# A decoder step on one core: the bank reads of four decays, low parts in quarters, and the place of three gate projections

## The chip, the core and the metric

The kernel runs on one core of a Trainium2 chip. What counts is its device time in microseconds (us). Before the change three runs took 1305.10, 1305.83 and 1306.04 us: a median of 1305.83.

The engines are named as in the profile: TensorE (PE, with its weight loads as PEld), VectorE (DVE), ScalarE (ACT), GpSimd (POOL) and SyncE (SP), which here issues DMAs. Each runs its own instructions in order and waits on semaphores for the others.

## What is computed

One layer of a hybrid decoder on 16 learned tokens, 256 prompt tokens and 8 sequences of 8 new tokens. All of them lie side by side as columns: 336 in a projection, of which 320 are kept as two chunks of 128 and a last strip of 64.

```python
def trunk_layer(x, conf_buf, mconv_buf, h0, segments, p):
    ...
    xn = rmsnorm(x, norm1_w)
    proj = xn @ w_in + b_in
    cuts = np.cumsum([2 * C_CONV, D_INNER, CONV_DIM, M_HEADS])
    glu_in, z, xbc, dt_raw, gate_raw = jnp.split(proj, [int(c) for c in cuts], axis=-1)

    ga, gb = jnp.split(glu_in, 2, axis=-1)
    u = ga * jax.nn.sigmoid(gb)
    conf_cat = jnp.concatenate([conf_buf.astype(u.dtype), u], axis=1)
    c = causal_depthwise(conf_cat, conf_dw_w, conf_dw_b)
    c = jax.nn.silu(layernorm(c, conf_ln_g, conf_ln_b))
    y_a = c @ w_conf_out + b_conf_out
    ...
    y = gated_group_rmsnorm(y.reshape(b, T, D_INNER), z, m_norm_w)
    y_b = y @ w_m_out

    g_a, g_b = jnp.split(jax.nn.sigmoid(gate_raw), 2, axis=-1)
    x = x + (g_a * y_a + g_b * y_b) @ w_o
    x = x + peer(rmsnorm(x, norm2_w), peer_w_q, peer_keys, peer_u, peer_v)
```

The `y` in the middle comes from a recurrence of 32 heads in 8 groups of 4. Within a chunk it is computed with a matrix of decays:

```python
        acs = jnp.cumsum(dtc * Ag, axis=1)
        seg = acs[:, :, None] - acs[:, None, :]
        decay = jnp.exp(jnp.where(causal[None, :, :, None, None], seg, -jnp.inf))
        cb = jnp.einsum('btgn,bsgn->btsg', Cc, Bc)
        dx = dtc[..., None] * xc
        y_diag = jnp.einsum('btsgr,bsgrp->btgrp', cb[..., None] * decay, dx)
        y_off = jnp.einsum('btgn,bgrpn->btgrp', Cc, hc) * jnp.exp(acs)[..., None]
        ...
        st = jnp.einsum('bsgn,bsgrp->bgrpn', Bc, w_end[..., None] * dx)
        h_new = jnp.exp(last)[..., None, None] * hc + st
```

`peer` is the expert stage: each token picks 16 of 16384 experts in each of 8 heads, and their rows of two tables are weighted and summed.

## The kernel before

**Weights.** A projection uses a weight block of 128x1024, fetched by SyncE into `wraw` (four buffers) and split in two: a high part `wh`, a copy by ScalarE (L243, "CAST"), and a low part `wl` = `wraw` - `wh`, by GpSimd (L247) or now and then by VectorE. `wh` and `wl` have two buffers each, so a block's parts are made while the projections before it still run. `proj` is 16 matmuls with `wh` (against the high and the low part of the activations, `ah` and `al`) and then 8 with `wl`. The results lie in banks named `pj`, three of them. `split` can cut the low part into `parts` pieces:

```python
                (nc.gpsimd if on_pool else nc.vector).tensor_tensor(l[:, q:q + m], src[:, q:q + m],
...
            split(h, l, raw, on_pool=not on_dve, on_dve=lm[0] == 1, parts=1 if lm[0] else 4)
```

`lm[0]` is the share of blocks whose low part VectorE makes. It is 0 in one stage alone, the projection `w_q` ahead of the experts: there, and nowhere else, GpSimd works in quarters.

**The mixer.** A loop goes over the eight groups g = 0 to 7. Each turn runs projections for the next group as tasks: the convolution branch's value and its gate half (`xnf` is the sigmoid of the gate half, `ccat` the product of both with its history, `ch` a copy of it for the convolution of 31 taps, which runs as pairs of a ScalarE product and a VectorE sum into `pcv`), four for x, B and C (`mcat`), then two for z (`sz`). After each task a generator of the group's recurrence, `ssd(g)`, takes one step, and the group before takes one of its last ones. The steps, with the names in the traces:

1. copies with `spread_in` (`ptr<-cst,spr`), `decay(0)`, `decay(1)`
2. `turn(0)`, `decay(2)`, `decay(3)`
3. `turn(1)`, `turn(2)`, small copies into `cz`
4. `running()`: `pq`, whose result ScalarE copies to `gs`, and `st` times `el` on GpSimd; `inner(0)`; `Bm`
5. `inner(1)`, `state(0)`; 6. `inner(2)`, `state(1)`; 7. `state(2)`, `out(0)`; 8. `out(1)`
9. the squares `sq` and the update of `st`; 10. the sum of squares `pgn`

`decay(r)` spreads one head's `acs` over 128 rows by a matmul into a bank `pdec` (L629). VectorE takes it in three pieces (64 or 128 columns, L631) into `dec`, ScalarE takes half of its rows into `e2` (`e` in the trace) with the exponential (L635), and after every second head ScalarE takes the exponential of a pair of `dec` in place (L637). `pdec` has two banks, shared with `py`, `po` and `pgb` (tag "y"). VectorE and ScalarE read a bank of `pdec` one after the other, in the order in which the program names them. `turn(i)` transposes three blocks into `ptr`, from which come `xt` and `wx`. `inner(i)` makes `pcb` and multiplies `dec` by it (L660, VectorE). `state(i)` makes `pst` and from it `hs`. `ptr`, `pq`, `pcb` and `pst` share two banks (tag "misc"): `pst` of `state(0)` takes the bank that the first `pcb` leaves, and `pq` that of the second `ptr`.

In the last turn (g = 7) eight gate projections take the place of the next group's tasks, with the convolution branch's layer norm between them: `norm_mean` and `norm_scale`, and `norm_apply`, where VectorE multiplies the buffers `cbuf` by `rs` (L841). `conf_out(0)` and `conf_out(1)` follow, with gates `gs`.

Behind the loop come the group norm's statistics, `conf_out(2)` to `(5)` (low parts on VectorE), and a loop over the groups: `gnorm` spreads a group's scale into a bank `pgb` and VectorE multiplies `xg` by it (L775, two instructions), `gsplit` cuts the result into `yh` and `yl`. `conf_out(6)` and `(7)` stand behind groups 1 and 3, and three gate projections behind the loop. Then `w_mo` (two blocks for an output), `w_o`, `w_q` and the expert stage: the tables' blocks `eraw`, read with 512 KB a DMA on two queues, go through TensorE (`in_uT`, L1417, then `in_vE`, L1519), while rows gathered by GpSimd's indirect DMAs (`wuv`) go through VectorE.

**What sets the order.** Up to the three gates each matmul is pinned, so TensorE keeps the program's order:

```python
        pin = [True]
        def mm(*a_, **kw):
            i_ = nc.tensor.matmul(*a_, **kw)
            if pin[0]:
                tc.keep_in_program_order(i_)
```

ScalarE's functions that need a table (`act`) are chained in the program's order too. All else is put in order by a scheduler. A function whose table isn't loaded gets an `ACT_TABLE_LOAD` ahead of it: the exponential and the sigmoid need different ones.

Of the kernel before, what the change touches and what calls it, by code (L numbers as in the profile page):

```python
# [61 lines left out]
NW0 = 3  # L62
# [96 lines left out]
def body(tc, ia, oa, stop=None):  # L159
    nc = tc.nc  # L160
    with ExitStack() as top:
# [13 lines left out]
# [4 lines that stand above are left out]
# [39 lines left out]
        def act(out, in_, f, **kw):  # L218
            i_ = nc.scalar.activation(out, in_, f, **kw)  # L219
            chain(i_)  # L220
            return i_
# [20 lines left out]
        def split(h, l, src, on_pool=False, on_dve=False, parts=1):  # L242
            (nc.vector.tensor_copy if on_dve else nc.scalar.copy)(h, src)  # L243
            n = src.shape[1]
            m = n // parts if on_pool and len(src.shape) == 3 else n
            for q in range(0, n, m):
                (nc.gpsimd if on_pool else nc.vector).tensor_tensor(l[:, q:q + m], src[:, q:q + m],  # L247
                                                                    h[:, q:q + m].bitcast(F32), op=OP.subtract)
# [22 lines left out]
        def weight(src, i):  # L271
            raw = wp.tile([128, KD, 128], F32, name="wraw", bufs=rb[0])
            nc.sync.dma_start(raw, src[i].rearrange("p (k m) -> p k m", m=128))
            h = wp.tile([128, KD, 128], F32R, name="wh", bufs=2)
            l = wp.tile([128, KD, 128], F32R, name="wl", bufs=2)
            nw[0] += 1
            f_ = lm[0]
            on_dve = int((nw[0] + 1) * f_) > int(nw[0] * f_)
            split(h, l, raw, on_pool=not on_dve, on_dve=lm[0] == 1, parts=1 if lm[0] else 4)
            return h, l  # L280

        lm, nw = [LM[3]], [NW0]

        def rows(h, l):
            return lambda k: (h[:, k, :], l[:, k, :])
# [331 lines left out]
        def ssd(g, xg, bc, sz):  # L617
# [8 lines left out]
            def decay(r):  # L626
                h = 4 * g + r
                pb = ps.tile([128, T], F32, name="pdec", tag="y", bufs=2)[:, :T2]
                mm(pb, id3[:, h:h + 1].to_broadcast([128, 128]), acs3[:, :T2], start=True, stop=True)  # L629
                for i, (t0, L) in enumerate(OTILES):  # L630
                    nc.vector.scalar_tensor_tensor(dec[:, r, t0:t0 + L], pb[:, t0:t0 + L], acs[i][:, h:h + 1],  # L631
                                                   mneg[:, t0:t0 + L], op0=OP.add, op1=OP.add)
                hs_ = slice(r % 2 * 64, r % 2 * 64 + 64)
                act(e2[hs_, r // 2], pb[hs_], AF.Exp)
                if r % 2:  # L635
                    act(dec[:, r - 1:r + 1], dec[:, r - 1:r + 1], AF.Exp)

# [80 lines left out]
            yield  # L718
            turn(0)
            decay(2)  # L720
            decay(3)
            yield
            turn(1)
            turn(2)
            for s_ in range(2):
                nc.scalar.copy(cz[:, 4 * s_:4 * s_ + 4, 8 * s_:8 * s_ + 8],
                               CT[:, SQ + 32 * s_:SQ + 32 * s_ + 32].rearrange("p (q t) -> p q t", q=4))
# [69 lines left out]
        def gate():  # L797
            n = len(gates)
            j = 2 * n if n < KD else 2 * (n - KD) + 1
            p = project(64 + j, xo)[:, :T2]  # L800
            s = gate_tile(n)
            nc.scalar.activation(s, p, AF.Identity, bias=V("b_in", 64 + j))  # L802
            gates.append(s)
# [74 lines left out]
        for g in range(G):  # L878
            new = ssd(g, *tiles, sz)
            if g + 1 < G:  # L880
                tiles, steps = xbc(g + 1)
                tasks = conf(g + 1) + steps
            else:
                lm[0] = LM[1]
                tasks = [gate] * 8
            run(old, 1)
            run(new, 1)
            for n, f in enumerate(tasks):
                f()
                run(old, 1)  # L890
                run(new, 1)
                if g + 1 == G:
                    if n == 0:
                        norm_mean()
                    elif n == 3:
                        norm_scale()
                    elif n in (4, 5):
                        norm_apply(range(4 * n - 16, 4 * n - 12))
            if g + 1 < G:
                sz, zsteps = zproj(g + 1)  # L900
                zsteps[0]()
                run(new, 1)
                zsteps[1]()
                old = new
            else:
                for j in range(2):
                    conf_out(j)
                    run(new, 1)
# [9 lines left out]
        for g in range(G):  # L918
            gnorm(g, r24[0])
            gsplit(g)  # L920
            if g % 2 and g < 4:
                conf_out(6 + g // 2)
        for _ in range(3):
            gate()
        pin[0] = False
        lm[0] = LM[2]
        mh = m2.tile([128, KD, T2], F32R, name="mh")
        ml = m2.tile([128, KD, T2], F32R, name="ml")

# [234 lines left out]
        for t in qTs:  # L1164
            nc.gpsimd.memset(t[:, T2:], 0.0)
        lm[0] = 0.0
        fetched = []
        pres = [ExitStack(), ExitStack()]

# [485 lines left out]
```

## Time and profile before

| | before |
|---|---|
| runs, median (lowest to highest) | 1305.83 us (1305.10 to 1306.04) |
| the profiled execution | 1305.18 us, of which the span is 1303.3 us |
| mean granted clock of TensorE | 0.993 |
| TensorE busy | 97% |
| VectorE, GpSimd, ScalarE busy | 74%, 45%, 40% |
| moved by DMA | 373.77 MB, 287 GB/s |

The span reaches from the first to the last instruction; 1.9 us of the execution lie around it. A percentage is an average over stages that differ: the mixer to about 430 us, where VectorE, ScalarE and GpSimd are all busy, then `w_mo`, `w_o` and `w_q`, and from about 800 us on the expert stage, in which the DMA engines are nearly full. In rows of the timeline a time is counted from the span's start, and in square brackets stands how long the engine had been idle and what released it.

### The profile page before, as it was taken

The numbers are of one execution on the slowest core, as the hardware profiler recorded it, in microseconds if no ns is written. First come the engines' busy times: TensorE is split into PE (matmuls) and PEld (weight loads), VectorE is DVE, ScalarE is ACT, GpSimd is POOL, SyncE is SP. The second block draws the span as 40 slices with busy tenths as digits, with TensorE's granted clock in tenths as the row PEclk, the third lists the DMA queues.
The fourth block names the chain that finished last, engine by engine and source line by source line (L and its number), as shares of the span: only waits on it lengthen the run. The fifth ranks groups of instructions, "written<-read, shape, count | busy, mean of one in ns | idle before, by whom it ended". The sixth has DMA issues, their size and how long they took to land.

```text
span 1303.3 us, 23601 instructions
## 1 busy us (share of the span) xinstructions
PE 1261.8 (97%) x8951; PEld 1216.5 (93%) x8951; DVE 961.0 (74%) x2095; ACT 521.9 (40%) x1332; POOL 584.2 (45%) x553
## 2 busy tenths in 40 slices
PE   9999999999889999999999899999999999999997
PEld 7989888898779999999999898999999999999997
DVE  6888778977987335548999967788788888544444
ACT  6878876787665444634222221112211111001102
POOL 2587777886673656975122222233332222122210
PEclk9999999999999999999999999899999999999999
DMA  6444454344424344765989999999999999999992
GB/s 247 172 145 160 169 187 166 137 168 154 148 95 160 138 149 146 262 228 187 379 321 416 415 415 415 415 412 416 414 415 415 414 415 415 397 416 415 413 411 110
DMA packets 85905, 373.77 MB, mean 287 GB/s; under 512 B 10000, under 2 KB 15376, under 8 KB 66208
## 3 DMA queue, kind: packets, MB, share of 16 engines
q1 hardware_dynamic: 48336, 166.82, 34.4%
q0 software_dynamic: 19584, 142.62, 26.7%
q10 hardware_dynamic: 17872, 62.84, 12.0%
q8 instruction: 70, 1.15, 0.3%
q14 instruction: 43, 0.35, 0.1%
HBM read 359.18 MB, written 13.06 MB: 286 GB/s over the span
## 4 chain that ended last, share of the span: by engine, by line
PE 81%; DMA 7%; DVE 7%; ACT 4%; issue 1%; POOL 0%; DVEq 0%; ACTq 0%; SPq 0%; POOLq 0%
PE pj L176 29%; PE va L1519 25%; PE pj L1417 17%; DMA eraw<-in_uT_dram 3%; DMA wuv<-in_peer_uv_dram,gid 3%; PE pg L1445 1%; PE pst L176 1%; ACT L219 1%; ACT wh L243 1%; PE po L176 1%; PE psc L1195 1%; DVE pcv L519 1%; PE py L176 1%; DVE st L712 1%; ACT e L219 1%
## 5 line engine op out<-in xcount | busy, mean ns | idle before, releaser
L1149 POOL DMA_INDIRECT wuv<-in_peer_uv_dram,gid x136 | 166.5, 1225 | 490.1 <-PE va L1519 118.8
L247 POOL TENSOR_TENSOR wl<-wraw,wh 128x1024 fp32r<-128x1024 f32 (+1 forms) x160 | 278.3, 1753 | 129.0 <-ACT wh L243 79.1
L1519 PE MATMUL va<-S,eraw 128*128 128x184 f32 x2048 | 325.6, 320 | 0.0
L1519 PEld LDWEIGHTS va<-S,eraw 128*128 128x128 f32 x2048 | 318.9, 190 | 0.9 <-issue 0.9
L1417 PE MATMUL pj<-nd,eraw 128*128 128x184 f32 x1792 | 293.5, 323 | 9.6 <-DMA eraw<-in_uT_dram 8.4
L1417 PEld LDWEIGHTS pj<-nd,eraw 128*128 128x128 f32 x1792 | 281.2, 191 | 11.1 <-issue 8.7
L176 PE MATMUL pj<-ah,wh 128*128 128x336 f32 (+1 forms) x768 | 241.8, 326 | 1.2 <-ACT gs L802 0.9
L176 PE MATMUL pj<-al,wh 128*128 128x336 f32 (+1 forms) x768 | 231.9, 315 | 0.0
L1315 DVE SCALAR_TENSOR_TENSOR ygat<-wuv,scg,ygat 128x1024 f32<-128x1024 f32 x128 | 164.0, 1281 | 90.8 <-ACT scg L1310 90.6
L1307 ACT ACTIVATE scg<-scg 128x1 f32<-128x1 f32 x136 | 27.3, 202 | 437.9 <-DVE wuv L1305 317.8
L1305 DVE SCALAR_TENSOR_TENSOR wuv<-wuv,x2m 128x1024 f32<-128x1024 f32 x128 | 156.3, 1221 | 48.8 <-DMA wuv<-in_peer_uv_dram,gid 47.9
L243 ACT CAST wh<-wraw 128x1024 fp32r<-128x1024 f32 x125 | 130.9, 1048 | 97.0 <-PE pj L176 78.9
L176 PEld LDWEIGHTS pj<-ah,wh 128*128 128x128 f32 x768 | 145.1, 189 | 7.0 <-issue 2.5
L176 PEld LDWEIGHTS pj<-al,wh 128*128 128x128 f32 x768 | 144.7, 189 | 0.7
L519 DVE SCALAR_TENSOR_TENSOR pcv<-ch,vec,pcv 128x320 f32<-128x320 f32 x232 | 127.7, 550 | 18.6 <-ACT pcv L517 16.0
L176 PE MATMUL pj<-ah,wl 128*128 128x336 f32 (+1 forms) x768 | 137.3, 315 | 0.0
L176 PEld LDWEIGHTS pj<-ah,wl 128*128 128x128 f32 x768 | 119.9, 188 | 0.6 <-POOL wl L247 0.3
L1419 ACT ACTIVATE S<-pj 128x184 f32<-128x184 f32 x128 | 37.8, 315 | 89.6 <-PE pj L1417 89.2
L530 DVE SCALAR_TENSOR_TENSOR pj<-mcat,vec,pj 128x360 f32<-128x360 f32 x96 | 56.5, 591 | 3.4 <-ACT pj L528 3.1
L219 ACT ACT_TABLE_LOAD x31 | 39.8, 1283 | 19.5 <-DVE dec L631 19.0
L1456 DVE SCALAR_TENSOR_TENSOR S<-pg,S 128x232 f32<-128x232 f32 (+1 forms) x92 | 34.7, 417 | 13.1 <-PE pg L1445 13.1
L1417 PE MATMUL pj<-nd,pre 128*128 128x184 f32 x256 | 42.0, 319 | 0.0
(388 smaller groups left out, 1701.8 us busy)
## 6 DMA issues: line engine op xcount, KB each, us to landing
wraw<-in_w_in_dram SPq DMA_DIRECT2D x80, 512.0 KB, 3.2
eraw<-in_vE_dram SPq DMA_DIRECT2D x64, 512.0 KB, 10.2
eraw<-in_vE_dram ACTq DMA_DIRECT2D x64, 512.0 KB, 10.3
eraw<-in_uT_dram SPq DMA_DIRECT2D x60, 512.0 KB, 10.2
eraw<-in_uT_dram ACTq DMA_DIRECT2D x52, 512.0 KB, 10.1
st<-in_state_dram SPq DMA_DIRECT2D x8, 1024.0 KB, 5.0
out_ssm_s_dram<-st SPq DMA_DIRECT2D x8, 1024.0 KB, 5.0
wraw<-in_w_mo_dram SPq DMA_DIRECT2D x16, 512.0 KB, 3.2
```

Source lines behind the costliest of these rows:

```text
L176: i_ = nc.tensor.matmul(*a_, **kw)
L219: i_ = nc.scalar.activation(out, in_, f, **kw)
L243: (nc.vector.tensor_copy if on_dve else nc.scalar.copy)(h, src)
L247: (nc.gpsimd if on_pool else nc.vector).tensor_tensor(l[:, q:q + m], src[:, q:q + m], h[:, q:q + m].bitcast(F32), op=OP.subtract)
L519: nc.vector.scalar_tensor_tensor(to, in_, sc, eights(acc), op0=OP.mult, op1=OP.add)
L530: nc.vector.scalar_tensor_tensor(o, cat[:, w:w + n], wv, o, op0=OP.mult, op1=OP.add)
L1149: i_ = nc.gpsimd.indirect_dma_start(out=u, out_offset=None, in_=ia["peer_uv"], in_offset=bass.IndirectOffsetOnAxis(ap=gid[:, c:c + 1], axi ...
L1305: nc.vector.scalar_tensor_tensor(u[:, :D], u[:, :D], 1.0, x2m if c < NPICK else x2e, op0=OP.mult, op1=OP.mult, accum_out=w)
L1315: nc.vector.scalar_tensor_tensor(a_, u[:, D:], scg[:, c:c + 1], a_, op0=OP.mult, op1=OP.add)
L1417: i_ = nc.tensor.matmul(p[:, :ND], raw[:, k, :], nd[:, k, :], start=(k == 0), stop=(k == KD - 1))
L1419: nc.scalar.activation(Sv(b), p[:, :ND], AF.Gelu)
L1519: i_ = nc.tensor.matmul(va[k // 2][:, k % 2], raw[:, k, :], Sv(b), start=(b == 0 and k % 2 == 0), stop=(b == 127), skip_group_check=True)
```

## The change

It has three parts and removes no matmul.

- In `decay` ScalarE's exponential into `e2` is named ahead of VectorE's three reads, and `decay(3)` moves from the second step of `ssd` to the third, behind `turn(1)` and `turn(2)`.
- The count of pieces of a low part is a variable, `quarters`: 1 at the start, 4 from the last group's tasks on, 1 again from `w_mo` on, and 4 as before at `w_q`.
- Of the three gate projections behind the norm's loop one now stands in it, behind group 5; the other two stand behind group 7, where they were.

```diff
-            split(h, l, raw, on_pool=not on_dve, on_dve=lm[0] == 1, parts=1 if lm[0] else 4)
+            split(h, l, raw, on_pool=not on_dve, on_dve=lm[0] == 1, parts=quarters[0])
...
-        lm, nw = [LM[3]], [NW0]
+        lm, nw, quarters = [LM[3]], [NW0], [1]
...
                 mm(pb, id3[:, h:h + 1].to_broadcast([128, 128]), acs3[:, :T2], start=True, stop=True)
+                hs_ = slice(r % 2 * 64, r % 2 * 64 + 64)
+                act(e2[hs_, r // 2], pb[hs_], AF.Exp)
                 for i, (t0, L) in enumerate(OTILES):
                     nc.vector.scalar_tensor_tensor(dec[:, r, t0:t0 + L], pb[:, t0:t0 + L], acs[i][:, h:h + 1],
                                                    mneg[:, t0:t0 + L], op0=OP.add, op1=OP.add)
-                hs_ = slice(r % 2 * 64, r % 2 * 64 + 64)
-                act(e2[hs_, r // 2], pb[hs_], AF.Exp)
                 if r % 2:
...
             turn(0)
             decay(2)
-            decay(3)
             yield
             turn(1)
             turn(2)
+            decay(3)
...
                 lm[0] = LM[1]
+                quarters[0] = 4
                 tasks = [gate] * 8
...
                 conf_out(6 + g // 2)
-        for _ in range(3):
-            gate()
+            elif g % 2:
+                for _ in range(g // 2 - 1):
+                    gate()
         pin[0] = False
         lm[0] = LM[2]
+        quarters[0] = 1
...
         lm[0] = 0.0
+        quarters[0] = 4
```

**ScalarE in one of the groups 0 to 6.** Before, from the third and fourth reads of `pdec` on:

```order
L219 ACTIVATE e_2774<-pdec 64x320 x2
L219 ACTIVATE dec<-dec 128x640
L243 CAST wh<-wraw 128x1024
L219 ACT_TABLE_LOAD
L219 ACTIVATE xnf<-pj,vec 128x336
L646 COPY xt_2933<-ptr 128x128
L646 COPY xt_2942<-ptr 128x128
L537 COPY cnew<-ccat 128x30
L499 COPY ch<-ccat 128x1216
L537 COPY cnew<-ccat 128x240
L501 COPY ch<-ccat 128x304
L243 CAST wh<-wraw 128x1024
```

And after, from the cast behind `Bm` on (the third read of `pdec` and three `Bm` stand ahead of it):

```order
L243 CAST wh<-wraw 128x1024
L219 ACT_TABLE_LOAD
L219 ACTIVATE xnf<-pj,vec 128x336
L646 COPY xt_2926<-ptr 128x128
L646 COPY xt_2935<-ptr 128x128
L219 ACT_TABLE_LOAD
L219 ACTIVATE e_2774<-pdec 64x320
L537 COPY cnew<-ccat 128x30
L499 COPY ch<-ccat 128x1216
L537 COPY cnew<-ccat 128x240
L501 COPY ch<-ccat 128x304
L219 ACTIVATE dec<-dec 128x640
```

The fourth read stands behind `xnf` and the copies of `xt`, with a table load of its own, and the exponential of the second pair of `dec` has come from ahead of `xnf` to behind the copies of `ch`. In the built program one table load has been added in each of the groups 0 to 6; the last group has no `xnf`.

**TensorE at the norm's spreads, groups 5 and 6.** Before (`acs_4957` is the scale that is spread, `id_566` the selector, and a gate projection is the row of `ah`, `al` and eight `wl`):

```order
L176 MATMUL pj<-ch,wl 128x320 x8
L176 LDWEIGHTS id_566
L176 MATMUL pgb<-acs_4957,id_566 128x320
L176 LDWEIGHTS id_566
L176 MATMUL pgb<-acs_4957,id_566 128x320
L176 LDWEIGHTS id_566
L176 MATMUL pgb<-acs_4957,id_566 128x320
L176 LDWEIGHTS id_566
L176 MATMUL pgb<-acs_4957,id_566 128x320
L176 MATMUL pj<-ah,wh 128x320
```

And after, from the end of the gate that now stands between them:

```order
L176 MATMUL pj<-ah,wl 128x320 x8
L176 LDWEIGHTS id_566
L176 MATMUL pgb<-acs_4987,id_566 128x320
L176 LDWEIGHTS id_566
L176 MATMUL pgb<-acs_4987,id_566 128x320
L176 MATMUL pj<-ah,wh 128x320
L176 MATMUL pj<-al,wh 128x320
```

The spreads of groups 4 and 5 follow `conf_out(7)`, then comes a whole gate projection, and those of groups 6 and 7 come behind it.

**GpSimd in the last group.** Before (`wx` and `hs` are those of `turn` and `state`, `st` is `running`'s):

```order
L650 TENSOR_TENSOR wx_4511<-xt_4508,wd 128x256
L650 TENSOR_TENSOR wx_4520<-xt_4517,wd 128x256
L681 TENSOR_TENSOR st<-st,el 128x256 x4
L247 TENSOR_TENSOR wl<-wraw,wh 128x1024
L681 TENSOR_TENSOR st<-st,el 128x256 x4
L247 TENSOR_TENSOR wl<-wraw,wh 128x1024
L669 TENSOR_TENSOR hs_4672<-hs_4620,el 128x256
L247 TENSOR_TENSOR wl<-wraw,wh 128x1024
L669 TENSOR_TENSOR hs_4730<-hs_4672,el 128x256
```

And after:

```order
L650 TENSOR_TENSOR wx_4510<-xt_4507,wd 128x256
L650 TENSOR_TENSOR wx_4519<-xt_4516,wd 128x256
L247 TENSOR_TENSOR wl<-wraw,wh 128x256 x4
L681 TENSOR_TENSOR st<-st,el 128x256 x8
L247 TENSOR_TENSOR wl<-wraw,wh 128x256 x4
L669 TENSOR_TENSOR hs_4687<-hs_4632,el 128x256
L247 TENSOR_TENSOR wl<-wraw,wh 128x256 x4
L669 TENSOR_TENSOR hs_4748<-hs_4687,el 128x256
```

Each low part is four instructions of 256 columns instead of one of 1024, and one of them has moved ahead of the eight `st`. Over the whole program GpSimd's 96 full low parts become 82, and its 64 quarters become 120: fourteen low parts are made in quarters that were not.

## The prediction, made before the changed kernel was run

> **What bounds the kernel now.** I read the page first, then TensorE's waits, then the timeline of one group, of the last group and of the norm spreads. The page's busy line and the list of who waited for whom (total, times, longest, in us) say how much there is to win:
>
> ```profile
> PE 1261.8 (97%) x8951; PEld 1216.5 (93%) x8951; DVE 961.0 (74%) x2095; ACT 521.9 (40%) x1332; POOL 584.2 (45%) x553
> PE pdec L176 <- ACT e L219: 8.9, 15, 1.6
> PE pj L1417 <- DMA eraw<-in_uT_dram: 8.4, 4, 3.9
> PE pq L176 <- DVE xt L647: 4.0, 4, 1.9
> PE pst L176 <- DVE dec L660: 2.7, 1, 2.7
> PE pgn L176 <- POOL sq L750: 2.1, 1, 2.1
> PE pgb L176 <- DVE xg L775: 1.9, 2, 1.3
> ...
> PE pj L176 <- ACT gs L802: 0.9, 1, 0.9
> ```
>
> TensorE is busy 1261.8 of 1303.3 us and its matmuls stay in program order in the mixer, so the time is its work plus its gaps, 41.5 us in all. Nothing in the change removes matmuls. It can win only the rows above outside the 8.4 (that one lies in the expert stage), 20.5 us together, and it pays in new gaps.
>
> **The waits for the decays.** The fifth group (g = 4) shows how the 8.9 us arise. Columns: start, length, engine, line, operation, and the idle time before it with its releaser.
>
> ```profile
> 217.29 1.50 DVE L631 SCALAR_TENSOR_TENSOR dec<-pdec,acs,mneg 128x64 f32<-128x64 f32 x6
> 217.97 0.49 PE L181 MATMUL ptr<-cst,spr 128*128 128x128 f32 x3
> 218.16 1.28 ACT L219 ACT_TABLE_LOAD   x1 [4.77 <-DVE dec L631]
> 219.45 0.89 ACT L219 ACTIVATE e<-pdec 64x320 f32<-64x320 f32 x2
> 219.94 0.30 PE L176 MATMUL pdec<-acs,id 128*128 128x320 bf16 x1 [1.48 <-ACT e L219]
> 220.39 0.30 PE L176 MATMUL pdec<-acs,id 128*128 128x320 bf16 x1 [0.16 <-ACT e L219]
> ```
>
> The four `pdec` results share two banks. VectorE reads the first two banks from 217.29; only after its first three reads does ScalarE load its table and read; the third `pdec` needs the first bank back. TensorE was ready at 218.46 and started at 219.94; the fourth repeats it with 0.16. Afterwards ScalarE does not wait for VectorE here: it sat idle for 4.77 us, so load and both reads end before 217.29, and the bank is free after VectorE's first three of six operations, 0.75 us, at 218.04, before 218.46. The fourth comes behind the next two transposes, when both banks have long been read. Of 8.9 us I take 7.5 as won: VectorE holds a backlog of convolution steps, TensorE will arrive a little sooner, and 0.2 us in each of seven groups may stay. Bounds: 8.9, and nothing.
>
> **What ScalarE then owes.** Its function for `xnf` needs another table than the exponential, so the fourth decay behind `xnf` costs one more load in each of seven groups (the last has no `xnf`): 7 x 1.28 = 9.0 us of ScalarE, 40% busy. On the path it is a longer chain, seen in the same group:
>
> ```profile
> 222.37 0.99 ACT L733 ACTIVATE Bm<-xt,cstm 128x128 f32<-128x128 f32 x3
> 224.13 0.74 ACT L219 ACTIVATE dec<-dec 128x640 f32<-128x640 f32 x1
> 224.78 1.04 ACT L243 CAST wh<-wraw 128x1024 fp32r<-128x1024 f32 x1
> 225.83 1.28 ACT L219 ACT_TABLE_LOAD   x1
> 227.13 0.54 ACT L219 ACTIVATE xnf<-pj,vec 128x336 f32<-128x336 f32 x1
> 228.36 1.21 ACT L499 COPY ch<-ccat 128x1216 f32<-128x1216 f32 x1
> 230.12 1.04 ACT L243 CAST wh<-wraw 128x1024 fp32r<-128x1024 f32 x1
> 231.07 0.61 ACT L517 ACTIVATE pcv<-ch,vec 128x320 f32<-128x320 f32 x1
> 232.18 0.41 DVE L660 TENSOR_TENSOR dec<-dec,pcb 128x256 f32<-128x256 f32 x1
> 234.18 0.60 PE L176 MATMUL pst<-wx,Bm 128*128 128x256 f32 x2
> ```
>
> ScalarE's first exponential follows VectorE's sixth operation (218.79) and ends at 219.5; a cast (1.04), a copy (0.25), the third read (0.43), `Bm` (0.99), a cast (1.04) and the load (1.28) bring `xnf` to about 224.6 instead of 227.13, with its projection done by 222.6. Then `xnf` and two copies (0.87, from 227.13 to the next start less the wait), load 1.28, fourth read 0.43, the copies up to the cast 2.0, exponential 0.74, cast 1.04, `pcv` 0.61, and VectorE's `pcv` step and multiply by `pcb` (0.9): end about 232.5. `pst` takes over the bank of that `pcb`; it moves from 234.18 to about 232.4 (1.6 us from the decays, 0.18 from `pq`). The margin is nothing: I charge 0.35 us for each of seven groups, **2.5 us**. Bounds: nothing, and the rival below. Queued behind ScalarE's exponential are the cast and `pcv`; a cast is used a whole projection later, so only `pcv`, and VectorE behind it, feel it.
>
> [...] The load of 1.28 us starts 0.01 after the cast ends and `xnf` 0.02 after the load, so a load costs its own length. [...]
>
> `xnf` coming sooner also brings `ccat` and the `xt` behind it forward. `pq` waits 2.1 us for `xt` in groups 0 to 6 (4.0 less the last group's 1.92) and one projection 0.9 for a gate copy behind these exponentials. Of these 3.0 I take **1.5**. Bounds 3.0, and nothing.
>
> **Low parts in quarters.** In the last group VectorE is the late one:
>
> ```profile
> 365.24 2.64 POOL L247 TENSOR_TENSOR wl<-wraw,wh 128x1024 fp32r<-128x1024 f32 x1
> 368.66 2.60 POOL L247 TENSOR_TENSOR wl<-wraw,wh 128x1024 fp32r<-128x1024 f32 x1
> ...
> 365.66 5.95 DVE L841 TENSOR_TENSOR cbuf<-cbuf,rs 128x320 f32<-128x320 f32 x3
> 371.53 0.68 DVE L660 TENSOR_TENSOR dec<-dec,pcb 128x512 f32<-128x512 f32 x1
> 372.12 2.09 DVE L841 TENSOR_TENSOR cbuf<-cbuf,rs 128x320 f32<-128x320 f32 x5
> 372.26 0.70 PE L176 MATMUL pst<-wx,xt 128*128 128x256 f32 x2 [2.72 <-DVE dec L660]
> L247 POOL TENSOR_TENSOR wl<-wraw,wh 128x256 fp32r<-128x256 f32 x64 | 46.8, 763 | 15.9 <-ACT sall L1197 11.7 <-ACT wh L243 3.0 <-ACT qT L1191 1.1
> L247 POOL TENSOR_TENSOR wl<-wraw,wh 128x1024 fp32r<-128x1024 f32 x96 | 231.5, 2413 | 113.1 <-ACT wh L243 76.1 <-PE pgb L176 20.3 <-PE pj L176 16.5
> ```
>
> [...] Three multiplies between quarters cost at most 3 x (0.42 + 0.76) = 3.5 in place of 5.95, so `dec` is 2.4 us sooner and most of the 2.72 goes; `xt`, behind two sums of 1.5 us each, gains about 1.5 of its 1.92. Of the 4.6 together I take **3.4**, since `po` will then wait about a microsecond for `hs`, which stands behind the other five multiplies. Bounds: 4.6, and a loss of 3.1 (the second rival). Four quarters take 3.05 instead of 2.41 us: fourteen low parts are quartered, 9.0 us of GpSimd, beside its idle time.
>
> The end of that group has another row, and the window behind it (its bounds, its length, busy time and instructions of the five engines, granted clock, DMA share, GB/s):
>
> ```profile
> 390.96 0.81 PE L176 MATMUL pgn<-sq,cstm 128*128 128x320 f32 x2 [2.12 <-POOL sq L750]
> 392.00:395.00 3.00, 3.00 (x13) 3.00 (x13) 0.92 (x3) 0.68 (x2) 0.00 (x0) 0.50 1.02 426
> ```
>
> `sq` stands behind a low part and a chain of VectorE, GpSimd and ScalarE. Both sides shift, so I win only **0.5** of 2.12. The clock of 0.50 for 3 us behind it costs 3 x 0.5 = 1.5 us; whether it comes back depends on that gap, so I take about half, **0.8**. Bounds: 3.6 for both, and nothing.
>
> **Gates between norm spreads.**
>
> ```profile
> 420.15 0.30 PE L176 MATMUL pgb<-acs,id 128*128 128x320 bf16 x1 [1.32 <-DVE xg L775]
> 421.07 0.30 PE L176 MATMUL pgb<-acs,id 128*128 128x320 bf16 x1 [0.62 <-DVE xg L775]
> 423.54 1.34 PE L176 MATMUL pj<-ah,wl 128*128 128x320 f32 x8
> ```
>
> Four spreads stand in a row on two banks. The gate behind them lasts from 421.2 to 424.9, 3.7 us. Put between the second and the third spread of the row, it lets VectorE read the banks meanwhile: **1.9** won. The gate's weight needs no more than the same low part as before, made two projections ahead. Bounds: 1.94, and nothing if its low part is late.
>
> **The sum**: 7.5 - 2.5 + 1.5 + 3.4 + 0.5 + 0.8 + 1.9 = 13.1 us. Then the expert stage: its order on TensorE, VectorE and ScalarE is redrawn, though nothing of it is in the edit. There the DMA runs full (1.02), and at first TensorE waits for blocks:
>
> ```profile
> 810.00:820.00 10.00, 6.06 (x27) 5.80 (x27) 9.27 (x18) 1.42 (x6) 2.62 (x2) 0.75 1.02 417
> ...
> 1000.00:1100.00 100.00, 100.00 (x816) 99.13 (x816) 83.83 (x148) 10.44 (x42) 25.61 (x22) 1.00 1.02 415
> ```
>
> Blocks are fetched as TensorE frees their buffers, so the stage starts sooner by what was won; the redrawn order may move these stalls by some 4 us either way, and I take zero. The profiled execution took 1305.18 us (its span and 1.9 around it): 1305.18 - 13.1 = 1292.1. It lies 0.65 below the median of the runs, 1305.83, so I forecast **1292.7**.
>
> **The rivals.**
> - *More than that* (12%): all 20.5 us go but a few, and the clock stays up: about 1285. For it speaks ScalarE's idle time; against it, that VectorE's backlog sets the next wait.
> - *The low part becomes late* (12%). Between quarters VectorE takes its turn, so one low part would last 3.05 + 4 x 0.42 = 4.7 us. Three of them stand close together from 360 to 371, and the tightest has 0.3 us to spare (made until 367.88, used as below): at the third TensorE waits up to 3 x 2.2 - 0.3 = 6.3 us. The sum is 6.8, the time 1299. Against it: GpSimd is busy 45% of the span.
>
> ```profile
> 368.20 1.34 PE L176 MATMUL pj<-ah,wl 128*128 128x320 f32 x8
> ```
>
> - *The decays become late* (16%). If ScalarE does not run ahead, load, read, sum, exponential (1.28 + 0.43 + 0.78 + 0.74 = 3.2) come on top of a chain that has no margin, and TensorE waits at `pst`. Each microsecond in seven groups costs 7: 0.7 late gives 1298, 1.4 late 1302.5; the gain is gone from 1.9 late; 2.5 late, most of the 3.2, gives 1310, **slower than before**. [...] About a third of this chance lies beyond 1303.
> - *The expert stage takes it back* (8%): if transfers there, not TensorE, set the end, it stays at 1303 to 1306. For it speaks the DMA share in both rows above, against it that TensorE is busy without a gap in the second.
>
> The forecast itself, 1288 to 1297, has 50%; 2% is for the rest. To leave out no more than a fifth the range takes in the first two rivals and the milder half of the third: 1284 to 1301. A measurement of this kernel tells about 0.2%, 2.6 us, from no change. Faster 0.84, same 0.08, slower 0.08.
>
> **What would show it.** Right: `pdec` under 2 us in TensorE's waits; `xnf` starting within 2.5 us of its projection's end; the multiplies of L841 near 1 us each; no wait of `pgb`. Wrong: new rows `pst` or `pcb` waiting for `dec` or `gs` in each group, `pj` waiting for `wl` around 360 to 370, or a stall for `eraw` beyond 12 us in the expert stage.

## The result, and the profile after

Five runs took 1295.63 to 1299.69 us, with a median of **1297.84**; the kernel before has 1305.84 over five runs. The ratio is **0.9939** (95% interval 0.9924 to 0.9953): 8.0 us, 0.6%, faster. The forecast was 1292.7 with a range from 1284 to 1301: the direction was right and the range held, but the gain is 5 us smaller than forecast. The profiled execution took 1297.84 us with a span of 1296.1, 7.2 less than the span before. Two executions among those below, one of the kernel before (2578 us) and one of e7_hs (3281 us), took twice as long or more, and the ratios leave them out.

TensorE's busy line and its waits in the changed kernel (total, times, longest, in us):

```profile
PE 1267.0 (98%) x8951; PEld 1220.6 (94%) x8951; DVE 953.3 (74%) x2095; ACT 531.7 (41%) x1339; POOL 599.2 (46%) x595
PE pj L1421 <- DMA eraw<-in_uT_dram: 9.7, 5, 3.7
PE pdec L176 <- DVE dec L633: 3.3, 6, 0.8
PE po L176 <- DVE hs L670: 2.4, 1, 2.4
...
PE pj L176 <- DVE cbuf L519: 1.2, 1, 1.2
PE pcb L176 <- DVE dec L660: 0.6, 1, 0.6
PE pgn L176 <- POOL sq L750: 0.5, 1, 0.5
PE pj L176 <- POOL wl L247: 0.4, 1, 0.4
```

TensorE's gaps fell from 41.5 us (1303.3 - 1261.8) to 29.1 (1296.1 - 1267.0): 12.4 won, almost exactly the 12.3 that the forecast had for gaps. But the same 8951 matmuls took 1267.0 us instead of 1261.8, so 5.2 us went back. Counted by the stages of the table below, 1.8 us of that lie ahead of the last group, where both profiles have one slow stretch (at 44 us): there TensorE waits in pieces too short for a row, as the account of the chain further down shows. Another 2.5 lie in the last group and the `conf_out` behind it and 1.1 in the blocks of `in_uT`; in these stages the changed kernel's profile has more time at a slower clock. Here are the slow stretches of the last group, as windows (bounds, length, busy time of the five engines, granted clock, DMA share, GB/s):

```profile
337.59:341.00 3.41, 1.49 (x8) 0.71 (x6) 3.41 (x13) 1.76 (x6) 2.34 (x5) 1.00 0.79 308
341.00:344.41 3.41, 3.41 (x14) 3.21 (x13) 2.85 (x9) 2.10 (x6) 0.53 (x1) 0.50 0.46 156
364.89:368.30 3.41, 1.68 (x18) 1.05 (x16) 3.41 (x5) 2.90 (x6) 2.94 (x4) 1.00 0.33 127
368.30:371.71 3.41, 2.74 (x11) 2.74 (x12) 3.41 (x7) 3.38 (x7) 2.72 (x4) 0.50 0.43 159
371.71:375.12 3.41, 3.41 (x14) 3.41 (x14) 2.83 (x5) 2.87 (x7) 3.33 (x4) 0.50 0.34 107
```

A window in which TensorE is busy for 1.49 of 3.41 us, and one with 1.68, are followed by one at a clock of 0.50, where a matmul takes longer (products of `pj` of 128x320 start 0.27 us apart there and 0.15 at full clock); the second stretch lasts two windows, until TensorE fills one. The kernel before had one such stretch in this part (behind `pgn`, in the prediction), and its longest gap had none:

```profile
367.89:371.30 3.41, 1.65 (x12) 1.38 (x10) 3.41 (x3) 1.66 (x3) 3.37 (x2) 1.00 0.46 154
371.30:374.71 3.41, 2.16 (x19) 1.47 (x20) 3.41 (x9) 3.07 (x6) 0.09 (x1) 1.00 0.40 154
388.37:391.78 3.41, 1.29 (x8) 0.87 (x7) 1.33 (x2) 2.25 (x3) 1.96 (x3) 1.00 0.63 157
```

The 2.72 us of `pst` (369.5 to 372.3) were cut by the line at 371.30, and the window with the larger part, busy for 1.65 us, was followed by one at full clock. So 1.65 to 1.68 lies at an edge; the last section has the counts.

How much of this belongs to the change is another question, since the stretches differ between executions of one kernel. The profile before has a mean clock of 0.993. Of 44 other executions of that kernel, those beside the experiments, 6 reach that, and their mean is 0.990. The ten executions of the changed kernel have a mean of 0.991. These means don't show that the change lowers the clock; the profile before was one with little time at 0.50.

Stage by stage, in us between matmul starts in the timelines (first to seventh `pgn`; to the eighth; to the first `pgb`; to the first product of `w_o`; first block of `in_uT` to first of `in_vE`), with the windows of 3.41 us at a clock of 0.50 from the groups to `w_o`. The rows below the second are the experiments described further down. The products of `in_uT` begin at 550 us in the kernel before, so the expert stage starts well ahead of the 800 us given above, and its waits for blocks lie between 699 and 816 us.

| kernel | groups 1 to 6 | last group | conf_out 1 to 5 | spreads, w_mo | in_uT blocks | windows at 0.50 |
|---|---|---|---|---|---|---|
| before | 244.5 | 50.1 | 19.8 | 95.0 | 405.0 | 1 |
| changed | 240.2 | 49.4 | 18.3 | 93.4 | 405.8 | 3 |
| e4_again | 240.1 | 48.0 | 18.3 | 93.4 | 402.4 | 2 |
| e1_decay | 240.0 | 47.7 | 18.3 | 96.5 | 405.7 | 3 |
| e5_first | 239.8 | 49.3 | 18.3 | 94.9 | 407.8 | 2 |
| e6_move | 250.1 | 49.6 | 18.3 | 96.5 | 405.7 | 2 |
| e2_quarters | 244.4 | 49.0 | 18.3 | 96.4 | 404.8 | 2 |
| e8_noq | 239.9 | 48.5 | 18.3 | 92.7 | 404.9 | 2 |
| e7_hs | 240.1 | 47.9 | 19.8 | 93.4 | 404.0 | 2 |
| e3_gates | 244.4 | 49.4 | 18.3 | 92.7 | 400.9 | 1 |
| e11_two | 239.7 | 48.4 | 18.3 | 92.7 | 404.4 | 0 |
| e12_swap | 245.3 | 48.4 | 18.3 | 92.7 | 405.8 | 2 |

### The profile page after: what moved, and what is told of

It reads as the page before. It is cut to its first block, busy times and chain, and to the rows that moved or that the text cites. A ratio compares the mean times of both kernels' runs of the same rounds, so it can differ in the third digit from the quotient of the medians.

```text
span 1296.1 us, 23646 instructions
## 1 busy us (share of the span) xinstructions
PE 1267.0 (98%) x8951; PEld 1220.6 (94%) x8951; DVE 953.3 (74%) x2095; ACT 531.7 (41%) x1339; POOL 599.2 (46%) x595
## 4 chain that ended last, share of the span: by engine, by line
PE 64%; DVE 19%; DMA 9%; ACT 5%; issue 2%; POOL 1%; DVEq 0%; SPq 0%; POOLq 0%; ACTq 0%
PE va L1523 25%; PE pj L176 23%; PE pj L1421 11%; DMA wuv<-in_peer_uv_dram,gid 6%; DVE pcv L519 5%; DMA eraw<-in_uT_dram 3%; DVE pj L530 2%; DVE ygat L1319 2%; PE pg L1449 2%; DVE wuv L1309 1%; DVE st L712 1%; ACT L219 1%; ACT wh L243 1%; DVE dec L633 1%; PE pw L176 0%
## 5 line engine op out<-in xcount | busy, mean ns | idle before, releaser
L1152 POOL DMA_INDIRECT wuv<-in_peer_uv_dram,gid x136 | 173.9, 1278 | 483.5 <-PE va L1523 149.2
L247 POOL TENSOR_TENSOR wl<-wraw,wh 128x256 fp32r<-128x256 f32 (+1 forms) x202 | 288.6, 1449 | 105.5 <-ACT wh L243 57.0
L176 PE MATMUL pj<-ah,wh 128*128 128x336 f32 (+1 forms) x768 | 244.7, 329 | 0.5 <-ACT xnf L219 0.3
L176 PE MATMUL pj<-al,wh 128*128 128x336 f32 (+1 forms) x768 | 234.5, 318 | 0.0
L219 ACT ACT_TABLE_LOAD x38 | 48.8, 1283 | 0.7
```

The costliest lines, as they stand in the source:

```text
L1152: i_ = nc.gpsimd.indirect_dma_start(out=u, out_offset=None, in_=ia["peer_uv"], in_offset=bass.IndirectOffsetOnAxis(ap=gid[:, c:c + 1], axi ...
```

## Experiments

A ratio is against runs of the kernel before on the same chip, with its 95% interval.

### The changed kernel again, and its parts alone

**e4_again** is the changed kernel, unchanged.

> The changed kernel itself, once more. Theory (clock by a fixed grid): the granted clock is decided in stretches of 3.41 us whose grid lies differently in every execution, so the same gaps of TensorE (0.8 at 338 us, 1.2 at 340, 2.4 at 367, 2 to 3.7 in the expert stage) come back within 0.3 us, but the stretches at 0.50 do not all come back at the same places; the executions spread over 1295 to 1300 us, and those with a higher mean clock are the faster ones (0.993 near 1295.6, 0.988 near 1298 to 1299.7). Rival (each gap over about 1.9 us always costs a stretch): the stretches at 341 and 368 us are there again, and all executions lie within 1 us of 1297.8.

Measured: 1293.26 to 1297.39 us, median 1295.03 beside 1304.28; ratio 0.9933 (0.9919 to 0.9947). The gaps came back to 0.1 us in the mixer. So did the stretches behind 340 and 367 us, but the second lasted one window instead of two, and the last group is 1.4 us shorter. In this execution the grid lay only 0.5 us later than in the first profile, so the rival isn't beaten in the mixer by this run; executions of one kernel do spread over 4 us.

**e1_decay** has the two edits of the decays alone.

```diff
+                act(e2[hs_, r // 2], pb[hs_], AF.Exp)
                 for i, (t0, L) in enumerate(OTILES):
...
-                act(e2[hs_, r // 2], pb[hs_], AF.Exp)
...
             decay(2)
-            decay(3)
             yield
             turn(1)
             turn(2)
+            decay(3)
```

> Only the two edits of the decays. Theory (the gaps that the trace of the changed kernel lacks belong to the part that named them): TensorE's wait for pdec falls from 8.9 to about 3.3 with VectorE as releaser, pq's waits in groups 0 to 6 (2.1) go, the last group keeps pst near 2.7, pq near 1.9 and pgn near 2.1, the spreads keep pgb 1.9; no wait at pst in groups 0 to 6; time 4 to 7 us shorter, 1299 to 1302. Rival (the longer chain on ScalarE takes the gain): pst or pcb wait for dec in each group by 0.5 to 2 us, time 1304 to 1310.

Measured: median 1299.25, ratio 0.9953 (0.9938 to 0.9968). Groups 1 to 6 are as short as in the whole change. `pdec` waits 3.3 us for VectorE, `pst` 2.4, and no row of `pst` or `pcb` comes back in every group (three groups have waits there, most of them too short for a row; see the longer chain below). Two things were not expected: `pq`'s 1.9 in the last group are gone without the quarters, and `pgn` fell to 0.2. Two windows at 0.50 followed the gap of `pst`, which straddled the grid in the kernel before, and one the `pgb` gaps.

**e2_quarters** has the quarters alone.

```diff
-            split(h, l, raw, on_pool=not on_dve, on_dve=lm[0] == 1, parts=1 if lm[0] else 4)
+            split(h, l, raw, on_pool=not on_dve, on_dve=lm[0] == 1, parts=quarters[0])
...
+                quarters[0] = 4
                 tasks = [gate] * 8
```

> Only the quarters. Theory: L841 near 0.9 us each instead of 1.98, pst's wait of 2.7 gone, pq's 1.9 smaller, and po waits 1.5 to 2.5 for hs instead of 0.3; the gaps shrink by 2 to 4 us and the clock may give or take 1.7 to 3.4: 1301 to 1306. Rival (the gain of the whole change comes from the quarters): 1298 to 1300. Rival (low parts late): pj waits for wl, 3 us or more, and 1306 to 1309.

Measured: median 1303.64, ratio 0.998 (0.9967 to 0.9994), so 2.6 us (0.8 to 4.3). The wait of `pst` has gone, and these rows of TensorE's waits in its place:

```profile
PE po L176 <- DVE hs L670: 2.0, 1, 2.0
...
PE pj L176 <- POOL wl L247: 1.1, 3, 0.4
```

The low parts are a little late, by 0.4 us at most, not by the 6.3 of the prediction's rival.

**e3_gates** has the gate between the spreads alone.

```diff
-        for _ in range(3):
-            gate()
+            elif g % 2:
+                for _ in range(g // 2 - 1):
+                    gate()
```

> Only the gate between the spreads. Theory: the two waits of pgb (1.9 together) go, and nothing else up to there changes; 1.5 to 1.9 us shorter, 1304. Rival (the wait moves to the first product of w_mo, which needs the norm's results): pj waits 1 us or more for yh or wl behind the gates, and the time stays at 1305.8.

Measured: median 1299.05, ratio 0.9959 (0.9945 to 0.9974): 3 to 7 us, more than the two waits of `pgb` can hold. `pgb` has no row any more, and the stage is 2.3 us shorter. Up to the spreads the instructions stand as in the kernel before. In its profile the blocks of `in_uT` take 4.1 us less (TensorE waits 4.2 us for them instead of 8.4) and the rest of the expert stage 2.2 more; the scheduler had redrawn that stage's order. How much of the surplus is that order and how much the executions' spread, one profile doesn't settle. By their ratios the three parts alone come to 6.1, 2.6 and 5.3 us, 14 together, where the whole, in e4_again beside the same runs, has 8.7; so what a part brings alone can't be added up.

### Which of the two decay edits does it

**e5_first** is the first half of e1_decay's diff, **e6_move** the second half.

> Only ScalarE's read ahead of VectorE's; decay(3) stays in the second step. Theory (both edits are needed, since VectorE is now the last reader of a bank and stands behind its backlog): the third pdec waits about 0.5 us in each group, and the fourth, right behind it, another 0.5 to 0.8, for VectorE's second three reads; pdec together 6 to 9 us with VectorE as releaser, no more table loads than before, and the groups 0 to 6 are 0 to 2 us shorter than before: 1302 to 1306 for a kernel before of 1304 to 1306. Rival (the order of the readers alone brings the gain, the move only a table load): pdec near 3, groups 4 us shorter or more, 1298 to 1300.

> Only the move of decay(3) to the third step; VectorE still reads first. Theory: the third pdec still waits about 1.1 us for ScalarE in each group, the fourth no longer has its 0.16; seven more table loads; pdec 6 to 8 us with ScalarE as releaser; the groups 0 to 6 within 1.5 us of before. Rival (the move brings the gain): pdec near 3 and the groups 4 us shorter.

Measured: e5_first 1300.81 beside 1306.03, ratio 0.9958 (0.9942 to 0.9975); e6_move 1315.72, ratio 1.0074 (1.0045 to 1.0103). My theory falls: ScalarE's reading first is enough for groups 1 to 6 (239.8 us, against 240.0 with both edits), and the move alone makes them 5.6 us longer. TensorE's waits in e5_first, then in e6_move:

```profile
PE pdec L176 <- DVE dec L633: 5.3, 11, 0.9
PE pq L176 <- DVE xt L647: 3.1, 4, 1.9
```

```profile
PE pdec L176 <- ACT e L219: 10.0, 7, 2.1
...
PE pj L176 <- ACT xg L219: 3.8, 2, 1.9
PE pst L176 <- ACT gs L679: 2.7, 5, 0.9
```

In e6_move ScalarE pays the seven further loads and still waits for VectorE ahead of each first read, so its whole chain is late, and TensorE waits for copies behind it (`xg`, `gs`): that is close to the prediction's rival of late decays. Where ScalarE runs ahead, the wait for VectorE ahead of the loads is gone, as its rows show for the kernel before, e6_move and the changed kernel (count, busy time, mean ns, idle time ahead of them and its releaser):

```profile
L219 ACT ACT_TABLE_LOAD x31 | 39.8, 1283 | 19.5 <-DVE dec L631 19.0
```

```profile
L219 ACT ACT_TABLE_LOAD x38 | 48.8, 1283 | 22.8 <-DVE dec L631 22.2
```

```profile
L219 ACT ACT_TABLE_LOAD x38 | 48.8, 1283 | 0.7
```

The loads still lengthen ScalarE's chain there. The groups come out equal because the move also shortens the waits for `pdec`, from 5.3 us in e5_first to 3.3 in e1_decay, and for `pq`.

### What bounds the last group

**e8_noq** is the changed kernel without the quarters (the diffs of e1_decay and e3_gates together). **e7_hs** is the changed kernel with one order forced on VectorE:

```diff
-                    nc.vector.tensor_tensor(h_, h_, p, op=OP.add)
+                    added[i] = nc.vector.tensor_tensor(h_, h_, p, op=OP.add).ins.name
...
-                nc.vector.tensor_tensor(cb[:, k, :T2], cb[:, k, :T2], normed[0], op=OP.mult)
+                m_ = nc.vector.tensor_tensor(cb[:, k, :T2], cb[:, k, :T2], normed[0], op=OP.mult)
+                if k > 3:
+                    tc.add_manual_dep(m_.ins, added[1], mybir.DependencyInfo(mybir.DependencyClass.NoSync,
+                                                                             mybir.DependencyReason.DATA),
+                                      reason="hs first")
```

> The changed kernel without the quarters: decays and gate only. Theory (the quarters swap the wait of pst for one of po and win nothing on balance): last group as in the run with the decays alone, pst waits 2.4 and po nothing; ratio against before 0.992 to 0.995. Rival (the quarters are worth the 3.4 us that the forecast gave them): ratio 0.9955 to 0.997.

> The changed kernel, and in the last group VectorE adds the first hs ahead of the last four multiplies of the norm (L841 there) instead of behind all eight. Theory (the wait of po for hs is VectorE's order, and through the clock it costs more than its 2.4 us): po waits under 0.5 us, the stretch at 0.50 behind it (368 us in the span) is gone, and the last group is 2 to 5 us shorter than in the changed kernel; against the kernel before a ratio of 0.988 to 0.992. Rival (the wait only moves, to conf_out's activations or xg, which the delayed multiplies feed): pj or py wait 1.5 us or more, ratio 0.993 as without the edit.

Measured: e8_noq 1297.25 beside 1306.03, ratio 0.9927 (0.991 to 0.9945); e7_hs 1297.7, ratio 0.9935 (0.9916 to 0.9954). Both equal the whole change within their intervals. The rows of TensorE's timeline, first of e8_noq and then of e7_hs:

```profile
368.70 0.70 PE L176 MATMUL pst<-wx,xt 128*128 128x256 f32 x2 [2.30 <-DVE dec L660]
```

```profile
373.74 0.77 PE L176 MATMUL py<-dec,xt 128*64 128x64 f32 x12 [2.07 <-DVE xg L697]
386.10 0.81 PE L176 MATMUL pgn<-sq,cstm 128*128 128x320 f32 x2 [2.37 <-POOL sq L750]
```

A gap of 2.1 to 2.4 us stands in the last group of each of these kernels: at `pst` without quarters, at `po` with them, at `py` and `pgn` once `po` is helped. The rival of e7_hs holds; the stretch at 0.50 behind `po` went, and another came behind `pgn`.

### The two edits that matter, and one more

**e11_two** is ScalarE's read first (e5_first) and the gate (e3_gates). **e12_swap** has in addition:

```diff
-            run(old, 1)
             run(new, 1)
+            run(old, 1)
             for n, f in enumerate(tasks):
```

> Only the order of the readers (ScalarE first) and the gate between the spreads; decay(3) stays in the second step, no new quarters. Theory (these two edits hold the whole gain; the move and the quarters bring nothing on balance): groups 0 to 6 shorter by 4 to 5 us, the last group's gaps by 4, pgb's 1.9 gone; ratio 0.991 to 0.995, as for the whole change. Rival (the move of decay(3) is worth its 1.6 us in the last group, and the quarters their part): ratio 0.9955 to 0.998.

> As the run before, and at the start of each group's turn the new group's first step comes ahead of the old group's update of st, so that VectorE reads pdec ahead of four additions to st. Theory (the rest of pdec's wait is VectorE's backlog): pdec falls below 1 us in groups 0 to 6, which are 2 to 4 us shorter than in that run; ratio 0.988 to 0.992. Rival (the banks of pst, now held longer, make the next projection wait): pj waits for st 0.5 us or more in each group and the groups are no shorter.

Measured: e11_two 1297.44 beside 1304.77, ratio 0.9948 (0.9936 to 0.9961); e12_swap 1302.5, ratio 0.998 (0.9971 to 0.9988). Two of the four edits bring 5 to 8 us; whether the others add up to 0.2%, the overlapping intervals leave open. In e11_two `pq` keeps the last group's 1.9 us, as in e5_first; with the move this row is gone. e12_swap does what it should for `pdec`, but groups 1 to 6 take 245.3 us instead of 239.7, since the additions to `st`, now later, hold up `pgn`:

```profile
PE pgn L176 <- DVE st L712: 6.7, 7, 1.3
...
PE pdec L176 <- DVE dec L633: 0.9, 2, 0.5
```

So VectorE's backlog is where the rest of `pdec` comes from, and it can't be had by that order. No version beat the changed kernel clearly.

### What lowers the clock

**e9_gap5** and **e10_gap3** are the kernel before with pauses of TensorE in `w_mo` and `w_o`, with five and with three copies:

```diff
+        def pause(p):
+            t = tp.tile([128, T], F32, name="yo", bufs=2)[:, :T2]
+            for _ in range(5):
+                nc.vector.tensor_copy(t, p)
+            mm(misc([128, 128], "pcb"), ident, t[:, :128], start=True, stop=True)
...
+            pause(p)
             nc.vector.tensor_tensor(gb, p, gb, op=OP.mult)
```

> The kernel before, with sixteen pauses of TensorE, one behind each output of w_mo and w_o: VectorE copies the product five times (about 0.47 us each) and a small matmul waits for it, so each pause is about 2.4 us. Theory A (the clock is decided on a grid of 3.413 us that starts with TensorE's first work, 37.55 us ahead of the first stretch at 0.50): a stretch at 0.50 begins only on that grid, and only behind a grid window in which TensorE was idle for more than about 1.8 us; a pause that a grid line cuts into two smaller parts brings none; so about 11 of the 16 bring one, and the idle time in the window foretells which. Theory B (the length of a pause decides alone): all sixteen or none bring a stretch, and it begins right behind the pause. Pauses cost 16 x 2.4 = 38 us, the stretches of A about 1.7 each, 19 more.

> The same with three copies: pauses of about 1.5 us. Theory A: no window of the grid holds 1.8 us of idle time, so no stretch at 0.50 between 440 and 545 us, and the kernel is longer by the pauses alone, 16 x 1.5 = 24 us. Theory B with a threshold under 1.5 us: sixteen stretches, and some 27 us more.

Measured, one execution each: 1363.95 and 1340.19 us beside 1304.77; more than pauses and stretches add up to; the order in these stages was pinned too, which may be the rest. Nearly all pauses were 2.8 and 1.7 us long, so a little longer than meant. Two equal pauses in e9_gap5's timeline of TensorE, and then the windows of the grid around them:

```profile
474.08 0.46 PE L176 MATMUL pcb<-yo,cst 128*128 128x128 f32 x2 [2.78 <-DVE yo L930]
487.89 0.46 PE L176 MATMUL pcb<-yo,cst 128*128 128x128 f32 x2 [2.78 <-DVE yo L930]
```

```profile
472.32:475.73 3.41, 1.65 (x12) 1.68 (x13) 2.75 (x7) 0.46 (x1) 1.46 (x1) 1.00 0.38 129
475.73:479.14 3.41, 3.41 (x25) 3.41 (x25) 0.14 (x1) 2.05 (x3) 0.95 (x1) 1.00 0.22 90
485.98:489.39 3.41, 1.50 (x11) 1.53 (x12) 2.75 (x7) 0.46 (x1) 1.61 (x1) 1.00 0.47 155
489.39:492.80 3.41, 3.41 (x15) 3.41 (x15) 0.29 (x1) 1.05 (x1) 0.00 (x0) 0.50 0.25 96
```

The first, cut by the line at 472.32, has 1.76 us in its larger part and brings nothing; the second has 1.91 in one window and brings a stretch. Five of e9_gap5's pauses brought one, all beginning on the grid, and none of e10_gap3's did. Theory B is out; A's count of eleven was too high, since its 1.8 us is near the edge.

## Why the prediction was right or wrong

**The waits for the decays** (7.5 taken): 5.6 came, from 8.9 to 3.3. The cause was read rightly, ScalarE behind VectorE on two banks, and e5_first and e6_move show it from both sides. What stayed is 0.5 us a group where I left 0.2, and the profile of the fifth group shows why:

```profile
216.58 0.80 DVE L633 SCALAR_TENSOR_TENSOR dec<-pdec,acs,mneg 128x64 f32<-128x64 f32 x3
217.75 0.80 DVE L633 SCALAR_TENSOR_TENSOR dec<-pdec,acs,mneg 128x64 f32<-128x64 f32 x3
218.58 0.74 ACT L219 ACTIVATE dec<-dec 128x640 f32<-128x640 f32 x1 [3.83 <-DVE dec L633]
224.01 0.54 ACT L219 ACTIVATE xnf<-pj,vec 128x336 f32<-128x336 f32 x1
226.19 0.43 ACT L219 ACTIVATE e<-pdec 64x320 f32<-64x320 f32 x1
228.52 0.74 ACT L219 ACTIVATE dec<-dec 128x640 f32<-128x640 f32 x1
231.21 0.41 DVE L660 TENSOR_TENSOR dec<-dec,pcb 128x256 f32<-128x256 f32 x1
```

ScalarE is long done with the banks, and waits 3.83 us for VectorE, which comes to them only at 216.58, behind other additions (e12_swap takes these away, and the wait with them). In this group the third `pdec` just gets through; six times it waits, up to 0.8 us.

**The longer chain** (2.5 charged): 1.9 came, more than the one row of `pcb` (0.6) shows. The same group in the changed kernel:

```profile
231.68 0.49 PE L176 MATMUL pcb<-bc 128*128 128x128 f32 x2 [0.55 <-DVE dec L660]
231.78 0.38 ACT L679 COPY gs<-pq 128x256 f32<-128x256 f32 x1
232.22 0.70 PE L176 MATMUL pst<-wx,Bm 128*128 128x256 f32 x2
```

The second `pcb` starts when the multiply of the first has ended (231.62), and `pst` when the copy `gs` has (232.16). So the banks are not handed on as told above and as I took it in the prediction: here the second `pcb` takes the bank that the first leaves, and `pst` that of `pq`. From the start of the last product ahead of this `pcb` to that of `pst` it is 0.37 us in every group of the kernel before and of e5_first. In the changed kernel it is 0.64, 0.98 and 1.41 us in the first, third and fifth group and 0.37 in the others: 1.9 us more, and e4_again and e1_decay repeat it within 0.1. Most of it has no row and counts as busy time. The price was near, but it falls on three groups and not evenly on seven. The chain itself came as worked out: the fifth group stands 1.0 us earlier than before (its `pgn` of the group ahead at 216.4 instead of 217.4), so `xnf` at 224.01 answers to 225.0 where I had 224.6, and the multiply's end at 231.62 to 232.6 where I had 232.5. Each extra load takes 1.28 us (38 loads, 48.8 us), and the next function starts right behind it: the fifth group's two loads start at 222.71 and 224.89, and `xnf` and `e` 0.02 us after their ends, at 224.01 and 226.19.

**`pq` and the gate copy** (1.5 of 3.0): all 3.0 came; neither has a row any more.

**Quarters** (3.4): this is the step that failed. "Three multiplies between quarters" did go as forecast, 2.81 us in place of 5.95 (1.98 each), and what followed took it back:

```profile
361.06 2.81 DVE L841 TENSOR_TENSOR cbuf<-cbuf,rs 128x320 f32<-128x320 f32 x3
364.39 4.19 DVE L841 TENSOR_TENSOR cbuf<-cbuf,rs 128x320 f32<-128x320 f32 x5
368.50 0.41 DVE L670 TENSOR_TENSOR hs<-hs,pst 128x256 f32<-128x256 f32 x1
368.97 0.80 PE L176 MATMUL po<-bc,hs 128*128 128x128 f32 x2 [2.40 <-DVE hs L670]
```

The five multiplies behind took 4.19 us instead of 2.09: GpSimd works beside them too (from 364.3 to 367.8), where in the kernel before its low part had ended at 371.26, ahead of the first of them at 372.12. One by one, the three multiplies that overlapped whole low parts of 2.64 and 2.60 us took 2.57, 0.90 and 2.64 us before; in the changed kernel the seven that overlapped quarters took 0.92 to 1.03. Without a low part beside it a multiply took 0.48 in both. The two low parts in quarters lasted 3.82 and 3.52 us, where the second rival had 4.7. No run shows the up to 0.76 us more a multiply that the 3.4 was worked out with; that was my estimate, and in its place the runs showed 0.44 to 0.55 more. The eight gained 1 us together, `hs` stands behind them all, and `po` waits 2.1 us more than before (2.4 instead of 0.3), not one. By the gaps it is 2.7 + 1.9 - 2.1 = 2.5, but e8_noq shows that the whole change without quarters is as fast, and e1_decay that `pq`'s 1.9 belong to the decays. On top of the other edits the quarters are worth nothing that can be measured. I priced the wait that went, and gave the next one, in a chain with no slack, one microsecond where 2.1 came. (The bound of a loss of 3.1 is 2.9 by the second rival's own sum, 3.4 - 6.3.)

**`pgn`** (0.5): 1.6 came, but not through the change alone. Up to the spreads e3_gates, e9_gap5 and e10_gap3 have the order of the kernel before, and there `pgn` waits 0.8 us in the first and has no row in the other two. In these executions the gap of `pst` did bring a stretch at 0.50, of one, two and two windows. That puts TensorE behind, so it comes to `pgn` later and has less to wait. In e3_gates:

```profile
373.60 1.13 PE L176 MATMUL pst<-wx,xt 128*128 128x256 f32 x2 [2.72 <-DVE dec L660]
391.61 0.81 PE L176 MATMUL pgn<-sq,cstm 128*128 128x320 f32 x2 [0.78 <-POOL sq L750]
```

From the seventh `pgn` to the first `pgb` these three take 67.7, 68.4 and 68.3 us, the profile before 69.9, and the two of the changed kernel 67.7 and 66.3. So a stretch ahead of `pgn` need not cost what it lasts, and against these executions the last group gained between nothing and 2 us.

**The slow clock** (+0.8): this failed too. I gave a chance to the end of one stretch and none to new ones. The gaps of `norm_mean` (0.76 at `pdec` and 1.16 for `cbuf`, both in one window) and of `po` each brought one, where the 2.72 us of `pst` had been cut by the grid; with the second of `po`'s windows that is two more in the mixer on balance, and one more window was lost in the blocks. In this pair of profiles they go with 2.5 and 1.1 us of busy time, 3.6 lost where I had 0.8 won. But that is mostly luck of the executions: with mean clocks of 0.990 before and 0.991 after, nothing shows a loss through the change. I had priced a stretch that one execution happened to have.

**The gate between the spreads** (1.9): right; `pgb` has no row, 2.3 us in e8_noq's stage, and 1.6 in the changed kernel, where a low part came 0.4 us late.

**The expert stage** (0, within 4): +0.8 us in the first profile and -2.6 in the second of the same kernel, for the blocks of `in_uT`.

That the rows' gaps came to 12.4, as forecast, was luck, since the errors cancelled: too much for `pdec`, quarters and `cbuf` (a wait of 1.2 that I didn't see), too little for `pq` and `pgn`, and most of the chain's 1.9 is not in those rows. Against the medians, the forecast without the 3.4 of the quarters and the 0.8 of the clock would have been 8.9 us, and 8.0 were measured; that the remaining terms are each right can't be told from that. Of the signs named, two came (L841 near 1 us each, no wait of `pgb`), and two were missed: `pdec` is 3.3 and not under 2, and `xnf` in the fifth group starts 2.54 us behind its projection's end, just beyond the 2.5.

## What to carry to other kernels

Where two engines read a bank in turn, let the one with idle time read first, and look whether the other then stands behind a backlog. An edit that removes a gap from a chain without slack moves the gap, so price the next link before the gain; leaving one edit out of the whole tells more than running it alone. Where TensorE is busy all the time, a gap can have two prices, its length and the clock behind it, and two gaps can share a window: those of 0.76 and 1.16 us at `norm_mean`, 1.92 together, were followed by a stretch at 0.50, while none of the 43 windows with 1.3 to 1.71 us of idle time was. A profile is one execution: compare its clock with that of others before booking a difference to the change.

## What the runs showed of the hardware

- **The clock's grid.** In fourteen profiles all stretches at 0.50 begin on lines 3.413 us apart, and full ones last one or two such windows. Of the windows at full clock behind the first 60 us, without those ahead of the stretch that ends each profile, all 36 with 1.96 us or more of idle TensorE (3.41 less its busy time) were followed by one at 0.50, of 35 with 1.72 to 1.95 us fifteen, and of 43 with 1.3 to 1.71 us none. The grid's first line lay at 4.6 to 7.2 us of the span, differently in each execution, which may be part of why executions of one kernel spread over some 4 us. TensorE's first matmul starts at 1.32 us in all fourteen, so the grid does not start with TensorE's first work, as the expectation of e9_gap5 had it.
- **Table loads on an engine that runs ahead.** Seven more loads, 9.0 us of ScalarE, left groups 1 to 6 where they were (240.0 us in e1_decay against 239.8 in e5_first), though the longer chain's 1.9 us at `pcb` and `pst` came with them, balanced by shorter waits elsewhere. With ScalarE behind VectorE, in e6_move, the same seven came with 5.6 us.
